# Seven half-width products for eight in w1 of the SwiGLU: Strassen's scheme on 18 of 22 feature tiles

## The chip, the cores and the metric

The kernel runs on one core of a Trainium2 chip. A core has engines that run side by side and wait for each other through semaphores: TensorE (PE in the profile; PEld is its weight load), VectorE (DVE), ScalarE (ACT), GpSimd (POOL) and the engine that issues most of the DMAs (SP). Matmul results land in PSUM, which is used here as eight banks of 128 x 512 fp32; everything else that is held on chip lies in SBUF. The metric is the device time of one execution in microseconds (us).

## The reference

One layer of a diffusion backbone over 512 tokens of width 1024: a modulated RMSNorm, two parallel token mixers (mLSTM and Hyena), a gated merge and an output projection with a residual; then the part that matters here:

```python
x = x + g1 * y
h2 = rmsnorm(x, norm2_g[l]) * (1.0 + sc2) + sh2
x = x + g2 * swiglu(h2, ffn_w1[l], ffn_w3[l], ffn_w2[l])
return rmsnorm(x, final_g)

def swiglu(h, w1, w3, w2):
    return (jax.nn.silu(h @ w1) * (h @ w3)) @ w2
```

Here w1 and w3 are 1024 x 2816 and w2 is 2816 x 1024; all data are fp32.

## The kernel before, in words

Everything is kept transposed: features on the 128 partitions, the 512 tokens along the free axis. The model width is 8 tiles (KT) of 128 features, the hidden width of the SwiGLU 22 tiles (FT).

Precision. Each fp32 operand is split into a rounded high part and the rest, hi and lo (`split`, L214 to L216: ScalarE copies hi, VectorE subtracts to get lo). A product is three matmuls, hi x hi, hi x lo and lo x hi, accumulated in PSUM (`mm3`, L233 to L236). `gemm` (L574) runs `mm3` over eight 128-row blocks: 24 matmuls of a 128 x 128 stationary block against 128 x 512 moving columns. `wsplit` (L240) loads a weight tile into a buffer "wr" and splits it into buffers "wh" and "wl"; each of these tags has four buffers.

Order. The program text lists the work; a planner fixes, before the run, the order of the instructions of each engine's queue. It takes from the instructions whose inputs and buffers are free by its own estimate the one that stands earliest in the text. `wsplit` runs under a raised priority: its load and split count as 600 instructions earlier. `behind()` ties a block's instructions behind an earlier matmul.

The stages around the change:

- The output projection. `out_tile` (L1478) forms x1 (the residual stream, 8 tiles of 128 x 512), which stays in the two big "K" buffers to the end of the kernel. The last four tiles are made for one half of the tokens and then for the other (`last_tile`, L1520: matmuls 256 columns wide).
- The second norm. `norm2(hf)` (L1526) scales x1 by the norm (L1534, into scratch), adds the shift on ScalarE for the high part of h2 (L1535) and on VectorE for its low part (L1539), one half of the tokens at a time.
- The lead. w1 and w3 of feature tiles 0 and 1 are multiplied half by half of the tokens, 256 columns wide (`high_first`, L1550; L1556).
- The feature loop (L1584). For each of the 22 tiles, `up` (L1576) gives the products with w1 and w3 (for tiles 0 and 1 those of the lead), then L1588 to L1590 form silu(a) * b, L1598 splits it into hi and lo, and `background()` does one step of the modulation vectors that are needed last (one weight load, one VectorE pass, L363 and L373).
- The w2 loop (L1614). For each of 8 output tiles three loads of w2, 66 matmuls over the 22 hidden tiles, then `out_tile` and the final scale; the last output tile is made in two halves of the tokens, each followed by the last norm and the store (`last_norm`, L1603).

PSUM is two sets of four banks: `bank(psG)` for the gemms, `bank()` (psH) for the rest.

Of the kernel before, what the change touches and what calls it, by code (L numbers as in the profile page):

```python
# [9 lines left out]
F32 = mybir.dt.float32  # L10
F32R = mybir.dt.float32r
AF = mybir.ActivationFunctionType
# [5 lines left out]
SEQ = 512  # L18
# [142 lines left out]
def build(nc, tc, I, out, dbg=None):  # L161
# [40 lines left out]
    def bank(p=None):  # L202
        return T(p or psH, [128, 512], F32, "bank")
# [10 lines left out]
    def split(hi, lo, x):  # L214
        act.activation(hi, x, AF.Copy)  # L215
        dve.tensor_sub(lo, x, hi.bitcast(F32))  # L216
# [16 lines left out]
    def mm3(o, wh, wl, xh, xl, first, last):  # L233
        pe.matmul(o, wh, xh, start=first, stop=False)  # L234
        pe.matmul(o, wh, xl, start=False, stop=False)  # L235
        return pe.matmul(o, wl, xh, start=False, stop=last)  # L236
# [3 lines left out]
    def wsplit(src, shape):  # L240
        n = int(np.prod(shape[1:]))
        raw = T(PW, [128, WMAX], F32, "wr")
        hi = T(PW, [128, WMAX], F32R, "wh", 4)
        lo = T(PW, [128, WMAX], F32R, "wl", 4)

        def view(t):
            v = t[:, :n]
            return v if len(shape) == 2 else v.rearrange("p (a b) -> p a b", a=shape[1])

        with tc.high_priority(PR[0]):  # L250
            if isinstance(src, list):
                for s, sl in src:
                    dma(view(raw)[:, :, sl], s)
            else:
                dma(view(raw), src)
            split(hi[:, :n], lo[:, :n], raw[:, :n])
        return view(hi), view(lo)
# [928 lines left out]
    def background():  # L1186
        next(later, None)
# [155 lines left out]
    def steps(n):  # L1343
        for _ in range(n):
            background()
# [73 lines left out]


    PF = st.enter_context(pool("pf", reuse_waits="tile"))
    BUFS["big"] = 36
    g1h = T(P0, [128, KT], F32, "g1h")
    g2h = T(P0, [128, KT], F32, "g2h")
    am2 = T(P0, [128, KT], F32, "am2")
# [52 lines left out]
    def out_tile(ps, n, d, g, c0, x, xo, acc):  # L1478
        sl = slice(c0, c0 + n)
        dve.scalar_tensor_tensor(xo[:, sl], ps[:, :n], g[:, d : d + 1], x[:, sl], op0=ALU.mult, op1=ALU.add)  # L1480
# [39 lines left out]
    def last_tile(hf, d):  # L1520
        wh, wl = ws[d - KT + LAST]
        ps = bank(psG)
        gemm(ps, wh, wl, [half(t, hf) for t in y[0]], [half(t, hf) for t in y[1]], 256)
        return out_tile(ps, 256, d, g1h, 256 * hf, xr[d], x1[d], acc1)

    def norm2(hf, cols):  # L1526
        with behind():
            rb = half_rms(cols)
        ts = []
        for k in range(KT):  # L1530
            if k % 2 == 0:
                pair = scr()
            ts.append(half(pair, k % 2))
            m = dve.scalar_tensor_tensor(ts[k], half(x1[k], hf), am2[:, k : k + 1], rb[:, :256], op0=ALU.mult, op1=ALU.mult)  # L1534
            act.activation(half(h2[0][k], hf), ts[k], AF.Identity, bias=modT[:, 3, k, 0:1])  # L1535
        with tc.issue_after(m.ins):
            for k in range(KT):
                hi = half(h2[0][k], hf).bitcast(F32)
                dve.scalar_tensor_tensor(half(h2[1][k], hf), ts[k], modT[:, 3, k, 0:1], hi, op0=ALU.add, op1=ALU.subtract)  # L1539
# [7 lines left out]
    norm2(0, cols)  # L1547
    for d in range(KT - LAST + 2, KT):
        sq1 = last_tile(1, d)
    def high_first(ps, wh, wl, hf):  # L1550

        n = 0
        for w, x in ((wh, 0), (wl, 0), (wh, 1)):
            for k in range(KT):
                n += 1
                m = pe.matmul(ps, w[:, k], half(h2[x][k], hf), start=n == 1, stop=n == 3 * KT)  # L1556
        tails.append(m.ins)

    ff = ([], [])
# [24 lines left out]
    for f in range(FT):  # L1584
        pa = up("w1", f)
        pb = up("w3", f)
        t = scr()
        act.activation(t[:], pa[:], AF.Tanh, scale=0.5)  # L1588
        dve.scalar_tensor_tensor(t[:], t[:], 1.0, pa[:], op0=ALU.add, op1=ALU.mult)
        dve.tensor_tensor(t[:], t[:], pb[:], op=ALU.mult)  # L1590
        if f < 4:
            pair = T(PT, [128, 2, SEQ], F32R, ("uh", "ul")[f % 2])
            hl = pair[:, 0], pair[:, 1]
        else:
            hl = big(), big()
        for i in range(2):
            ff[i].append(hl[i])
        split(hl[0][:], hl[1][:], t[:])  # L1598
        background()
    dve.tensor_scalar_mul(g2h[:], modT[:, 5, :, 0], 0.5)  # L1600
    acc2 = scr()

# [8 lines left out]
    def half2(o, d, hf):  # L1611
        return o[:, d : d + 2, 256 * hf : 256 * hf + 256]

    for d in range(KT):  # L1614
        ws = []
        for k0 in (0, 8, 16):
            n = min(8, FT - k0)
            wh, wl = wsplit(I["w2"][d, :, k0 : k0 + n], [128, n, 128])
            ws += [(wh[:, k], wl[:, k]) for k in range(n)]
        for c0, n in ((0, SEQ),) if d < KT - 1 else ((0, 256), (256, 256)):  # L1620
            ps = bank(psG)
            sl = slice(c0, c0 + n)
            for k in range(FT):
                mm3(ps[:, :n], ws[k][0], ws[k][1], ff[0][k][:, sl], ff[1][k][:, sl], k == 0, k == FT - 1)
            sq = out_tile(ps, n, d, g2h, c0, x1[d], x1[d], acc2)
            act.activation(x1[d][:, sl], x1[d][:, sl], AF.Copy, scale=fing[:, d : d + 1])
            if n < SEQ:
                last_norm(c0 // 256, sq)
    st.close()
# [16 lines left out]
```

## Time and profile before

| | |
|---|---|
| median of 3 runs | 1216.29 us (1215.84 to 1220.05) |
| the profiled execution | 1217.14 us, its span 1215.2 us |
| mean granted TensorE clock | 0.995 |
| busy share of the span | PE 97%, PEld 83%, DVE 69%, ACT 43%, POOL 7% |
| second norm and lead | to 864.7 us |
| feature loop beyond the lead | 864.7 to 1082.3 us |
| w2 loop, last norm | 1082.3 to 1215.2 us |

The span is the time from the first instruction to the last. In rows of the timeline the columns are start and duration in us, the engine, the line of the kernel, the operation, its output and input by the program's names, and in brackets the idle time before it and what ended that. The duration of one row overlaps the start of the next on the same engine, so the cost of an instruction in a busy stretch is the distance of the starts.

### The profile page before, as it was taken

What the parts mean: (1) busy time and instruction counts of PE and PEld (TensorE: products, weight loads), DVE (VectorE), ACT (ScalarE), POOL (GpSimd) and SP (SyncE); (2) the same over time, 40 slices, a digit from 0 to 9 for tenths busy, and PEclk for the clock granted to TensorE, in tenths of its full rate; (3) what the DMA queues carried; (4) which work ended last, traced back from release to release, by engine and by line L of the source; (5) the groups of instructions that cost most, each with busy time, mean ns of one, the idle gap of its engine ahead of it and who ended that gap; (6) DMA issues with size and microseconds to landing.
All of it is one profiled execution on the core that took longest, in us unless ns stands there. A gap on an engine that the chain in (4) does not pass through costs nothing.

```text
span 1215.2 us, 16927 instructions
## 1 busy us (share of the span) xinstructions
PE 1180.2 (97%) x6488; PEld 1014.5 (83%) x6488; DVE 833.1 (69%) x1338; ACT 528.6 (43%) x825; POOL 88.4 (7%) x168
## 2 busy tenths in 40 slices
PE   4999999999999999999999999999999999999997
PEld 2799988888888888888889898779988888888886
DVE  6967797978989999898668786776753434432332
ACT  3754465753545444454666542233432232322221
POOL 0011110100010010101032221000000000000000
PEclk9999999999999999999999999999999999999999
DMA  9744353364244352435575677783543323233312
GB/s 349 247 161 161 137 184 106 135 240 141 74 161 139 127 177 94 150 112 176 200 235 196 204 234 251 257 286 97 153 151 104 93 99 102 85 95 96 96 48 70
DMA packets 63377, 189.04 MB, mean 156 GB/s; under 512 B 8760, under 2 KB 12608, under 8 KB 61120
## 3 DMA queue, kind: packets, MB, share of 16 engines
q1 hardware_dynamic: 51536, 150.20, 38.1%
q0 software_dynamic: 11760, 37.76, 8.7%
q8 instruction: 51, 0.84, 0.3%
q14 instruction: 30, 0.25, 0.1%
HBM read 154.37 MB, written 33.55 MB: 155 GB/s over the span
## 4 chain that ended last, share of the span: by engine, by line
PE 82%; DVE 8%; DMA 5%; issue 2%; ACT 2%; POOL 0%; SPq 0%; DVEq 0%; POOLq 0%; ACTq 0%
PE bank L234 23%; PE bank L235 23%; PE bank L236 23%; DMA wr<-in_wada 2%; PE bank L661 2%; PE bank L660 2%; PE bank L662 2%; PE bank L1556 2%; DMA wr<-in_wph 1%; DVE wl L216 1%; DVE wr L373 1%; PE bank L617 1%; PE bank L464 1%; PE bank L465 1%; DMA ul<-in_xT 1%
## 5 line engine op out<-in xcount | busy, mean ns | idle before, releaser
L234 PE MATMUL bank<-hTh,wh 128*128 128x512 f32 x896 | 351.1, 393 | 2.0 <-ACT hTh L1112 2.0
L235 PE MATMUL bank<-hTl,wh 128*128 128x512 f32 x896 | 350.6, 391 | 2.2 <-DVE hTl L1118 2.2
L236 PE MATMUL bank<-hTh,wl 128*128 128x512 f32 x896 | 350.1, 391 | 0.0
L215 ACT ACTIVATE wh<-wr 128x1024 fp32r<-128x1024 f32 (+1 forms) x167 | 172.2, 1032 | 406.4 <-PE bank L235 197.9
L216 DVE TENSOR_TENSOR wl<-wr,wh 128x1024 fp32r<-128x1024 f32 (+1 forms) x167 | 198.1, 1189 | 172.9 <-ACT wh L215 171.4
L234 PEld LDWEIGHTS bank<-hTh,wh 128*128 128x128 f32 x896 | 168.8, 188 | 35.9 <-ACT hTh L1112 2.2
L235 PEld LDWEIGHTS bank<-hTl,wh 128*128 128x128 f32 x896 | 168.8, 188 | 35.5 <-DVE hTl L1118 2.5
L236 PEld LDWEIGHTS bank<-hTh,wl 128*128 128x128 f32 x896 | 168.7, 188 | 34.4
L234 PE MATMUL bank<-big,wh 128*128 128x512 f32 (+1 forms) x274 | 97.0, 354 | 1.3 <-ACT big L215 1.3
L235 PE MATMUL bank<-big,wh 128*128 128x512 f32 (+1 forms) x274 | 97.0, 354 | 0.6 <-DVE big L216 0.6
L236 PE MATMUL bank<-big,wl 128*128 128x512 f32 (+1 forms) x274 | 96.6, 353 | 0.0
L234 PEld LDWEIGHTS bank<-big,wh 128*128 128x128 f32 x274 | 52.1, 190 | 8.6 <-ACT big L215 1.7
L235 PEld LDWEIGHTS bank<-big,wh 128*128 128x128 f32 x274 | 52.3, 191 | 8.0 <-DVE big L216 1.1
L373 DVE SCALAR_TENSOR_TENSOR wr<-wr,crow 128x1024 f32<-128x1024 f32 x32 | 38.9, 1220 | 29.0 <-DMA wr<-in_wada 29.0
L236 PEld LDWEIGHTS bank<-big,wl 128*128 128x128 f32 x274 | 52.3, 191 | 6.9
L215 ACT ACTIVATE hb<-hb 128x512 fp32r<-128x512 f32 (+1 forms) x49 | 36.6, 768 | 32.2 <-DVE hb L469 17.5
L1590 DVE TENSOR_TENSOR s<-s,bank 128x512 f32<-128x512 f32 x22 | 15.1, 686 | 48.1 <-PE bank L236 48.1
L392 POOL TENSOR_TENSOR rr<-rv,negh 128x2 f32<-128x2 f32 (+1 forms) x6 | 5.5, 924 | 511.3 <-DVE rv L390 511.3
L216 DVE TENSOR_TENSOR hb<-hb,hb 128x512 fp32r<-128x512 f32 (+1 forms) x49 | 40.5, 860 | 2.0 <-ACT hb L215 1.8
L660 PE MATMUL bank<-wh,hTh 128*128 128x256 f32 (+1 forms) x128 | 36.5, 285 | 0.0
L662 PE MATMUL bank<-wh,hTl 128*128 128x256 f32 (+1 forms) x128 | 36.5, 285 | 0.0
L661 PE MATMUL bank<-wl,hTh 128*128 128x256 f32 (+1 forms) x128 | 36.4, 284 | 0.0
(390 smaller groups left out, 2259.7 us busy)
## 6 DMA issues: line engine op xcount, KB each, us to landing
wr<-in_win SPq DMA_DIRECT2D x64, 512.0 KB, 4.0
wr<-in_w SPq DMA_DIRECT2D x60, 512.0 KB, 3.6
wr<-in_wada SPq DMA_DIRECT2D x32, 512.0 KB, 4.2
Kd<-K POOLq DMA_DIRECT2D x8, 1024.0 KB, 4.7
K<-Kd SPq DMA_DIRECT2D x8, 1024.0 KB, 6.4
wr<-in_wv SPq DMA_DIRECT2D x8, 512.0 KB
gmd<-s POOLq DMA_DIRECT2D x16, 256.0 KB, 2.6
wr<-in_wph SPq DMA_DIRECT2D x8, 512.0 KB, 3.9
```

Of the source, the lines that this page charges most:

```text
L215: act.activation(hi, x, AF.Copy)
L216: dve.tensor_sub(lo, x, hi.bitcast(F32))
L234: pe.matmul(o, wh, xh, start=first, stop=False)
L235: pe.matmul(o, wh, xl, start=False, stop=False)
L236: return pe.matmul(o, wl, xh, start=False, stop=last)
L373: dve.scalar_tensor_tensor(w, w, 1.0, crow[:], op0=ALU.mult, op1=ALU.mult, accum_out=s)
L464: pe.matmul(ps[:], lhs, w4h, start=True, stop=False)
L660: pe.matmul(o, xh, wh, start=bool(k == 0), stop=False)
L661: pe.matmul(o, xh, wl, start=False, stop=False)
L662: m = pe.matmul(o, xl, wh, start=False, stop=bool(k == KT - 1))
L1556: m = pe.matmul(ps, w[:, k], half(h2[x][k], hf), start=n == 1, stop=n == 3 * KT)
L1590: dve.tensor_tensor(t[:], t[:], pb[:], op=ALU.mult)
```

## The change

w1 of feature tiles 4 to 21 is done in nine pairs of tiles. The product of a pair is seen as a 2 x 2 block product: two feature tiles (rows of the result) by two halves of the tokens (columns), summed over two halves of the 1024 inputs. Strassen's scheme in the form with common sub-sums (Winograd's) needs seven block products where the plain way needs eight; each block product is four 128-row blocks, three matmuls each, 256 columns wide.

- `input_sums` (once, after feature tile 1) forms the four sums of quarter blocks of h2 from the scaled values, which `norm2` now leaves in eight buffers (`scaled`), and splits them into hi and lo.
- `weight_sums` (each pair) loads the two w1 tiles, forms four sums of weight blocks in place, and splits the seven stationary blocks: p (A11, A12), q (A22), u (S3, S4), v (S1, S2). These four take all four buffers of "wh" and "wl". It is not under the raised priority.
- `pair_up` runs the seven products into four banks of psH and puts the results together: one copy on ScalarE, four sums on VectorE, into a "K" buffer.
- silu(a) * b is kept unsplit (`raw`) and split later: four tiles within the feature loop, the other 18 (`ff_split`) in the w2 loop.
- The first two output tiles of w2 are done together, hidden tile by hidden tile, into two banks.
- x1 is stored to DRAM (`x1d`) and loaded back in the w2 loop, so that the "K" buffers are free between. The tag "big" has 38 buffers in place of 36. `background()` runs once a pair.

w3, feature tiles 0 to 3 and the output tiles 2 to 7 are computed as before.

```diff
+    x1d = T(PD, [128, KT, SEQ], F32, "x1d")
...
     def project(d, ps):
         out_tile(ps, SEQ, d, g1h, 0, xr[d], x1[d], acc1)
+        store(x1d[:, d], x1[d])
...
+    scaled = [big(F32) for _ in range(KT)]
...
-        ts = []
+        ts = [half(t, hf) for t in scaled]
...
+    store(x1d[:, KT - LAST :], xq[1][:])
...
+    def input_sums():
+        sh = modT[:, 3, :, 0]
+        dsh = T(PF, [128, KH], F32, "dsh", 1)
+        dve.tensor_sub(dsh[:], sh[:, KH:], sh[:, :KH])
+        for k in range(KH):
+            (l0, l1), (h0, h1) = ([half(scaled[j], i) for i in range(2)] for j in (k, k + KH))
+            dve.tensor_sub(l0, l1, l0)
+            dve.scalar_tensor_tensor(l1, h1, dsh[:, k : k + 1], l1, op0=ALU.add, op1=ALU.subtract)
+            dve.scalar_tensor_tensor(h1, h1, sh[:, k + KH : k + KH + 1], l0, op0=ALU.add, op1=ALU.subtract)
+            dve.scalar_tensor_tensor(h0, h0, sh[:, k + KH : k + KH + 1], h1, op0=ALU.add, op1=ALU.subtract)
...
+        for k in range(KT):
...
+            split(hi, lo, scaled[k_][:])
...
+    def weight_sums(n, f):
...
+        dma(r1[:, : 2 * H], I[n][f].rearrange("p a b -> p (a b)"))
+        dma(r2[:, : 2 * H], I[n][f + 1].rearrange("p a b -> p (a b)"))
+        a11, a12, a21, a22 = r1[:, :H], r1[:, H : 2 * H], r2[:, :H], r2[:, H : 2 * H]
...
+        p, q, u, v = pair(), pair(), pair(), pair()
+        split(p[0][:, : 2 * H], p[1][:, : 2 * H], r1[:, : 2 * H])
+        split(q[0][:, :H], q[1][:, :H], a22)
+        dve.tensor_tensor(a11, a11, a21, op=ALU.subtract)
+        dve.tensor_tensor(a21, a21, a22, op=ALU.add)
+        dve.tensor_tensor(a22, a22, a11, op=ALU.subtract)
+        dve.tensor_tensor(a12, a12, a22, op=ALU.subtract)
+        split(u[0][:, : 2 * H], u[1][:, : 2 * H], r1[:, : 2 * H])
+        split(v[0][:, : 2 * H], v[1][:, : 2 * H], r2[:, : 2 * H])
...
+    def pair_up(n, f, ts):
+        w = weight_sums(n, f)
...
+        b = [bank() for _ in range(4)]
+        for a, x, o in (("a11", b11, half(b[0], 0)), ("a12", b21, half(b[1], 0)), ("a22", ts[3], half(b[2], 0)), ("s3", ts[2], half(b[3], 0)),
+                        ("s4", b22, half(b[3], 1)), ("s1", ts[0], half(b[2], 1)), ("s2", ts[1], half(b[1], 1))):
+            for k in range(KH):
+                m = mm3(o, w[a][0][k], w[a][1][k], x[0][k], x[1][k], k == 0, k == KH - 1)
...
+        act.activation(c[:, 6], half(b[0], 0), AF.Copy)
+        dve.tensor_tensor(c[:, 0:5:4], two(b[1]), twice(6), op=ALU.add)
+        dve.tensor_tensor(c[:, 5:7], two(b[3]), twice(4), op=ALU.add)
+        dve.tensor_tensor(c[:, 2:4], two(b[2]), twice(5), op=ALU.add)
+        dve.tensor_tensor(c[:, 1], half(b[2], 1), c[:, 6], op=ALU.add)
...
+    for f in range(LEAD, FT, 2):
+        t = [silu_half(a) for a in pair_up("w1", f, ts)]
+        b = [up("w3", f + i)[:] for i in range(2)]
+        for i in range(2):
+            gated(t[i], b[i])
+        if early < EARLY and f > LEAD:
+            for _ in range(1):
+                ff_split(early, big()[:], big()[:])
+                early += 1
         background()
...
+    pair = [bank() for _ in range(2)]
+    for k0 in (0, 8, 16):
+        ws = [w2_part(d, k0) for d in range(2)]
+        for k in range(k0, min(k0 + 8, FT)):
+            if ff[0][k] is None:
+                ff_split(k, *next(free))
+            for d in range(2):
+                m = mm3(pair[d][:], *ws[d][k - k0], ff[0][k][:], ff[1][k][:], k == 0, k == FT - 1)
+        if k0 < 16:
+            reload_x1(k0 // 8)
```

In the w2 loop the split parts of hidden tiles 4 to 11 go to the buffers of h2 (`hTh`, `hTl`), those of 12 to 17 to "big", those of 18 to 21 to "uh" and "ul".

More of the change, by code (lines that the diff above doesn't have):

```diff
@@ L1557, in high_first @@
         tails.append(m.ins)
-    ff = ([], [])
+    ff, raw = ([None] * FT, [None] * FT), []
     lead = {}
@@ L1585, in build @@
+    LEAD, EARLY = 4, 4
+    for f in range(LEAD):
         pa = up("w1", f)
         pb = up("w3", f)
[L1587 to L1595, printed above, removed]
-        for i in range(2):
-            ff[i].append(hl[i])
@@ L1600, in build, with places @@
+    def places():
+        for _ in range(KT):
+            yield slots("hTh")()[:], slots("hTl")()[:]
+        for _ in range(FT - EARLY - KT - 4):
+            yield big()[:], big()[:]
+        for _ in range(2):
+            u, v = (T(PT, [128, 2, SEQ], F32R, t) for t in ("uh", "ul"))
+            for j in range(2):
+                yield u[:, j], v[:, j]
+    free = places()
+    x1.clear()
+    xq = [T(PT, [128, 4, SEQ], F32, "K") for _ in range(2)]
     dve.tensor_scalar_mul(g2h[:], modT[:, 5, :, 0], 0.5)
@@ L1612, in half2, with w2_part, reload_x1, down_tile @@
         return o[:, d : d + 2, 256 * hf : 256 * hf + 256]
[L1614 to L1619, printed above, removed]
+    def w2_part(d, k0):
+        n = min(8, FT - k0)
+        wh, wl = wsplit(I["w2"][d, :, k0 : k0 + n], [128, n, 128])
+        return [(wh[:, k], wl[:, k]) for k in range(n)]
+    def reload_x1(i):
+        store(xq[i][:], x1d[:, 4 * i : 4 * i + 4])
+        x1.extend(xq[i][:, j] for j in range(4))
+    pair = [bank() for _ in range(2)]
[8 more added lines that the diff above has]
+            reload_x1(k0 // 8)
+    tails.append(m.ins)
+    def down_tile(d, ps, c0, n):
+        sl = slice(c0, c0 + n)
+        sq = out_tile(ps, n, d, g2h, c0, x1[d], x1[d], acc2)
+        act.activation(x1[d][:, sl], x1[d][:, sl], AF.Copy, scale=fing[:, d : d + 1])
+        return sq
+    for d in range(2):
+        down_tile(d, pair[d], 0, SEQ)
+    for d in range(2, KT):
+        ws = [w for k0 in (0, 8, 16) for w in w2_part(d, k0)]
         for c0, n in ((0, SEQ),) if d < KT - 1 else ((0, 256), (256, 256)):
```

51 lines of the change are left out of this document (43 added, 8 removed).

## The prediction

> **What bounds the kernel now.** I read the page first: the busy shares, then the chain that ended last.
>
> ```profile
> span 1215.2 us, 16927 instructions
> PE 1180.2 (97%) x6488; PEld 1014.5 (83%) x6488; DVE 833.1 (69%) x1338; ACT 528.6 (43%) x825; POOL 88.4 (7%) x168
> PE 82%; DVE 8%; DMA 5%; issue 2%; ACT 2%; POOL 0%; SPq 0%; DVEq 0%; POOLq 0%; ACTq 0%
> ```
>
> TensorE carries 82% of the chain. The shares are means over stages, so the second view is the busy time in stretches: the half-width products of the output projection, the feature loop, and the w2 loop (columns: stretch, length, busy time and count of PE, PEld, DVE, ACT, POOL, granted clock, DMA share, GB/s).
>
> ```profile
> 822.00:836.00 14.00, 14.00 (x120) 14.00 (x119) 6.50 (x14) 4.05 (x8) 1.74 (x1) 1.00 0.12 39
> 865.00:1082.00 217.00, 217.00 (x959) 179.74 (x958) 92.95 (x113) 62.58 (x80) 0.00 (x0) 1.00 0.36 111
> 1082.00:1195.00 113.00, 113.00 (x532) 94.94 (x531) 34.11 (x36) 30.48 (x36) 0.00 (x0) 1.00 0.25 73
> ```
>
> In the feature and w2 loops PE has no gap at full clock, while VectorE is busy 43% and 30% of the time. So time is won there by taking matmul time away and lost by making PE wait. The third view is the order in time, for the pace. One turn of the feature loop on VectorE:
>
> ```profile
> 1049.90 0.69 DVE L1590 TENSOR_TENSOR s<-s,bank 128x512 f32<-128x512 f32 x1 [2.70 <-PE bank L236]
> 1050.81 1.22 DVE L216 TENSOR_TENSOR wl<-wr,wh 128x1024 fp32r<-128x1024 f32 x1 [0.23 <-ACT wh L215]
> 1051.95 0.69 DVE L216 TENSOR_TENSOR big<-s,big 128x512 fp32r<-128x512 f32 x1
> 1056.25 1.23 DVE L216 TENSOR_TENSOR wl<-wr,wh 128x1024 fp32r<-128x1024 f32 x1 [3.61 <-ACT wh L215]
> 1057.39 0.68 DVE L1589 SCALAR_TENSOR_TENSOR s<-s,bank 128x512 f32<-128x512 f32 x1
> 1060.78 0.69 DVE L1590 TENSOR_TENSOR s<-s,bank 128x512 f32<-128x512 f32 x1 [2.70 <-PE bank L236]
> ```
>
> L1590 waits for the second gemm of a turn, and it comes every 10.88 us: 48 matmuls of 512 columns, 0.2267 us each. VectorE has two waits of 2.7 and 3.6 us in each turn. The half-width pace is read from the output projection's last tiles, where L1480 waits for a gemm of 24 matmuls of 256 columns:
>
> ```profile
> 821.14 0.49 DVE L1480 SCALAR_TENSOR_TENSOR K<-bank,g1h,big 128x256 f32<-128x256 f32 x1 [1.42 <-PE bank L236]
> 824.02 0.49 DVE L1480 SCALAR_TENSOR_TENSOR K<-bank,g1h,big 128x256 f32<-128x256 f32 x1 [1.48 <-PE bank L236]
> 826.90 0.48 DVE L1480 SCALAR_TENSOR_TENSOR K<-bank,g1h,big 128x256 f32<-128x256 f32 x1 [1.42 <-PE bank L236]
> ```
>
> 2.88 us for 24 is 0.120 us each: more than half of 0.2267 (0.1133). That surcharge eats much of what one product in eight saves. Each of these gemms has new weights, bank and waits, and the pace is still 2.88, so the start of a product costs nothing visible.
>
> **The change, part by part.**
>
> *Removed and added on PE.* Before, w1 of two tiles: 48 x 0.2267 = 10.88 us. After: 7 products x 4 blocks x 3 = 84 half-width matmuls, 84 x 0.120 = 10.08 us. Nine pairs save 9 x 0.80 = 7.2 us. w3 and w2 keep their matmuls.
>
> By the Trainium skill, "TensorE: Matmul & The Clock Gate", section "Back-to-back issue gap", a warm matmul of N columns is spaced N/2.4 + 2.5 ns: 215.8 and 109.2 ns, and the sum by it would be 9 x (48 x 0.2158 - 84 x 0.1092) = 10.7 us, an estimate. The trace's spacings are 11 ns above both; I go by the trace.
>
> *VectorE and ScalarE in a pair.* Distances of starts in busy stretches give the cost:
>
> ```profile
> 850.40 3.22 DVE L1534 SCALAR_TENSOR_TENSOR s<-K,am,bank 128x256 f32<-128x256 f32 x8 [1.70 <-PE bank L394]
> 853.54 3.25 DVE L1539 SCALAR_TENSOR_TENSOR hTl<-s,modT,hTh 128x256 fp32r<-128x256 f32 x8
> ...
> 898.32 1.23 DVE L373 SCALAR_TENSOR_TENSOR wr<-wr,crow 128x1024 f32<-128x1024 f32 x1 [3.17 <-DMA wr<-in_wada]
> 899.47 0.08 DVE L373 DVE_READ_ACCUMULATOR wr<-wr,crow 128x1 f32 x1
> 899.47 1.22 DVE L216 TENSOR_TENSOR wl<-wr,wh 128x1024 fp32r<-128x1024 f32 x1
> 900.61 0.68 DVE L1590 TENSOR_TENSOR s<-s,bank 128x512 f32<-128x512 f32 x1
> 901.20 0.16 DVE L376 TENSOR_TENSOR modT<-modT,vecs 128x8 f32<-128x8 f32 x1
> ```
>
> 1024 columns cost 1.14 us, 512 cost 0.6, 256 cost 0.4 (3.22 / 8). A pair then takes of VectorE: lo of p, q, u, v 3 x 1.14 + 0.6 = 4.0; four weight sums 2.4; two w3 tiles 2.3; four output sums 3 x 0.6 + 0.4 = 2.2; silu and gate 2.4; one early split 0.6; one modulation pass 1.2. That is 15.1 us in a pair of 10.08 + 10.88 = 20.96 us: 72%. No row shows a sum in place, or one that writes two separate blocks; the nearest, which reads a bank with a repeated operand (L1608), has 682 ns, as L1590 has without one (686). So I take the single cost; double, as the upper bound, adds 2.4 + 2.2 and gives 19.7 us, still under 20.96. On ScalarE the 1024-column copy has a mean of 1.06 us:
>
> ```profile
> L216 DVE TENSOR_TENSOR wl<-wr,wh 128x1024 fp32r<-128x1024 f32 x39 | 47.8, 1225 | 61.4 <-ACT wh L215 61.4
> L215 ACT ACTIVATE wh<-wr 128x1024 fp32r<-128x1024 f32 x39 | 41.4, 1061 | 139.0 <-issue 135.4 <-PE bank L235 2.0 <-PE bank L1556 0.8
> L1588 ACT ACTIVATE s<-bank 128x512 f32<-128x512 f32 x20 | 11.6, 582 | 0.0
> ...
> L1590 DVE TENSOR_TENSOR s<-s,bank 128x512 f32<-128x512 f32 x22 | 15.1, 686 | 48.1 <-PE bank L236 48.1
> L1608 DVE TENSOR_TENSOR s<-K,bank 128x512 f32<-128x512 f32 x8 | 5.0, 682 | 3.3 <-PE bank L394 3.3
> ```
>
> At most 5 x 1.06 + 6 x 0.6, 9 us of 20.96. All of it lies beside PE: cost 0 if the order lets it. If that cover goes, the price is the first rival below.
>
> *Weight buffers in a pair.* The order of needs is p, q, u, v, then w3 tiles a, b, with four buffers. If the buffers go round in this order, the next p and q take those of u and v, free when the seven products end, 10.9 us before they are needed. The next u takes a's, free 5.4 us before the pair starts; the next v takes b's, free only at its start, and is ready some 1.06 + 1.14 = 2.2 us later; it is read by the sixth product, 5 x 1.44 = 7.2 us in. a and b take p's and q's, free 2.9 and 4.3 us in, needed at 10.1. Nothing is late. That buffers go round in the text's order, whatever the priority, I read from the load queue, where the unraised modulation loads stand between the raised w1, w3 loads, one for each turn:
>
> ```profile
> 859.93 0.33 SPq L363 DMA_DIRECT2D wr<-in_wada  x1
> 861.67 3.03 SPq L255 DMA_DIRECT2D wr<-in_w  x2
> 866.72 0.33 SPq L363 DMA_DIRECT2D wr<-in_wada  x1
> 867.86 4.85 SPq L255 DMA_DIRECT2D wr<-in_w  x2
> ```
>
> *The first pair.*
>
> ```profile
> 864.71 0.40 PE L234 MATMUL bank<-hTh,wh 128*128 128x512 f32 x1
> ...
> 867.75 0.68 DVE L1590 TENSOR_TENSOR s<-s,bank 128x512 f32<-128x512 f32 x1
> ```
>
> From the end of norm2 (853.54 + 3.25 = 856.8) VectorE has until s3 is read. PE runs tiles 2 and 3 plainly from 864.7 for 4 x 5.44 us, to 886.4, and reaches s3 at 886.4 + 3 x 1.44 = 890.7. Work due by then: silu and gate of tiles 0 to 2 and the first half of 3, 4.2; four plain weight tiles 4.6; input sums 16 x 0.4 + 8 x 0.6 + 0.2 = 11.4; p, q, sums and u 5.2. Together 25.4 of 33.9 us. I take 0; if the planner starts the input sums only after the gate of tile 1 (868.4 in this trace) they end at 879.8 and u still fits. Bound 0 to 2 us.
>
> *w2, first two tiles together.* 132 matmuls either way, 29.9 us. The splits moved here take 0.6 on VectorE and ScalarE per hidden tile against 6 x 0.2267 = 1.36 on PE; four are made before, so the fifth is due 5.4 us in, and its buffer falls free in the last w3 gemm. Cost 0. Without that head start the first would cost about 1.2 us once.
>
> *x1 through DRAM.* Five stores and two loads on POOL's queue.
>
> ```profile
> 71.57 0.72 POOL L509 DMA_DIRECT2D Kd<-K  x1 [10.35 <-DVE K L508]
> ...
> 853.19 1.72 PE L1556 MATMUL bank<-hTh,wh 128*128 128x256 f32 x13
> ...
> 848.78 0.70 POOL L392 TENSOR_TENSOR rr<-rv,negh 128x2 f32<-128x2 f32 x1 [16.22 <-DVE rv L390]
> Kd<-K POOLq DMA_DIRECT2D x8, 1024.0 KB, 4.7
> ```
>
> The 1 MB store becomes ready some 846 us in and holds POOL about 0.7 us; the power of the second norm (L392), queued behind it, is due at 848.8, and PE's wait behind that is covered until 853.2, when it turns to the second half of the tokens. Cost 0; at worst 0.7. The loads back have 15 us and more for 4.7.
>
> *Sum.* 1217.14 (the profiled execution, 1.9 above its span) - 7.2 = 1209.9. The median, 1216.29, is 0.85 lower: 1209.1 us. A median run can tell some 0.5%, 6.1 us, from no change, so the gain stands only 1.1 us beyond that.
>
> **The rivals.**
>
> *First, slower: the weight sums come late in every pair.* They are not raised, and stand in the text after the gate of the pair before, which waits for the last w3 gemm. If VectorE kept the text's order, PE would wait at each pair's start for that gate and lo of p, 0.6 + 1.14, and again at s3: p, q, four sums end 4.8 us in, hi of u 5.8, lo 7.0, when PE has been ready since 1.7 + 4.3 = 6.1. That is 2.6 us a pair, 9 x 2.6 = 24, net 17: 1233 us. It costs the gain from 0.8 us a pair on, and decides for "slower" from 1.5. Against it:
>
> ```profile
> 845.41 1.22 DVE L373 SCALAR_TENSOR_TENSOR wr<-wr,crow 128x1024 f32<-128x1024 f32 x1
> ...
> 846.89 1.22 DVE L373 SCALAR_TENSOR_TENSOR wr<-wr,crow 128x1024 f32<-128x1024 f32 x1
> ```
>
> These two passes belong to the feature loop (eight L373 rows from here on are its eight) and are not raised, yet run before the norm2(1) rows at 850.4, which stand earlier in the text. Work that is ready is drawn ahead. For the rival: the planner goes by its own estimate of durations, and its queues don't change when the chip is otherwise.
>
> *Second, same: the order is right but for single waits* at the first pair, at v, or at the start of w2, together 2 to 5 us: 1211 to 1214, say 1213. For it: VectorE goes from 43% to 72%, and every buffer of "wh" is in use.
>
> *Third, faster still:* the surcharge of half-width matmuls is not theirs but due to a stream in those stretches (PEld is busy 14.00 of 14.00 there) and absent here. Then 84 x 0.1133 = 9.52 us a pair, 9 x 1.36 = 12.2: 1204. Against it: the same 0.120 in all the half-width gemms.
>
> *Fourth: the change doesn't do what it says*, since the larger "big" tag moves buffers and the planner orders earlier stages otherwise:
>
> ```profile
> 700.00:818.00 118.00, 114.70 (x590) 97.53 (x589) 89.58 (x177) 37.62 (x58) 12.53 (x23) 0.99 0.76 256
> ```
>
> PE idles 3.3 us in the stage before the half-width products, so I give this 3 us either way, inside the range and within the cases above.
>
> **How the numbers follow.** Forecast 0.48 (its own range 1208.5 to 1211, from -7.7 to -5.3), third rival 0.04, second rival 0.32, first 0.16, of which a quarter is a light form (1 us a pair, 1218). Faster: 0.04 and all of the forecast but some 0.02 that falls short of 6.1 us, and a few hundredths of the second: 0.52. Slower 0.14, same 0.34. Range 1207 to 1222: it leaves out the third rival and the heavy part of the first, 0.17.
>
> **What would show it.** Right: in the feature loop PE busy throughout, turns of 20.96 us per pair, 84 half-width matmuls in 10.08; VectorE near 72% there; the w2 loop starting 7.2 us earlier and as long as before. Wrong: idle PE at the start of a pair with VectorE's weight split as the releaser (first rival), idle PE once near 886 to 895 or at the start of w2 (second), 0.113 per half-width matmul (third).

## The result, and the profile after

The changed kernel takes 1210.22 us (median of 6 runs, 1209.88 to 1210.75), the kernel before beside it 1216.07 us (6 runs, 1214.89 to 1220.05). The ratio of the means is 0.9945, with a 95% interval from 0.9927 to 0.9963: 0.55% faster, 4.5 to 8.9 us. The forecast was 1209.1 us, 7.2 us less than before.

The page of the changed kernel: span, busy shares, and the chain that ended last.

```profile
span 1208.6 us, 17766 instructions
PE 1174.4 (97%) x6812; PEld 1024.5 (85%) x6812; DVE 901.4 (75%) x1453; ACT 552.6 (46%) x860; POOL 92.2 (8%) x175
PE 85%; DVE 6%; DMA 5%; issue 2%; ACT 1%; POOL 0%; SPq 0%; DVEq 0%; POOLq 0%; ACTq 0%
```

TensorE has 324 matmuls more, 9 x (84 - 48), and is busy 5.8 us less. VectorE has 68 us of work more, and its share of the chain fell from 8% to 6%: the added sums are not on the path that sets the end.

The busy time of the changed kernel in stretches (columns as in the prediction): the feature loop, the seven products of the first pair, the two w3 tiles behind them, and most of the w2 loop.

```profile
865.00:1075.00 210.00, 210.00 (x1283) 189.32 (x1282) 155.93 (x217) 82.92 (x107) 1.11 (x2) 1.00 0.39 127
886.52:896.59 10.07, 10.07 (x85) 10.06 (x84) 7.14 (x8) 4.62 (x5) 0.00 (x0) 1.00 0.76 237
896.59:907.50 10.91, 10.91 (x50) 9.02 (x49) 7.89 (x13) 2.85 (x4) 0.00 (x0) 1.00 0.21 70
1075.00:1190.00 115.00, 115.00 (x549) 96.91 (x548) 41.24 (x50) 35.13 (x47) 0.00 (x0) 1.00 0.26 82
```

PE has no gap in either loop, at full clock. The 84 half-width matmuls take 10.07 us, 0.120 us each, and the two w3 tiles 10.91. In one pair VectorE is busy 7.14 + 7.89 = 15.03 of 20.98 us, 72%.

The pace of the pairs is read from ScalarE's copy of the first product (L1671), which comes once a pair. These are its rows in the first two pairs and the last:

```profile
888.15 0.38 ACT L1671 ACTIVATE K<-bank 128x256 f32<-128x256 f32 x1 [0.54 <-PE bank L236]
909.13 0.38 ACT L1671 ACTIVATE K<-bank 128x256 f32<-128x256 f32 x1 [0.54 <-PE bank L236]
...
1055.99 0.38 ACT L1671 ACTIVATE K<-bank 128x256 f32<-128x256 f32 x1 [0.54 <-PE bank L236]
```

(1055.99 - 888.15) / 8 = 20.98 us a pair, and the first is no different from the rest. Before, two feature tiles took 21.76 us.

The first matmuls of the feature loop and of the w2 loop, in the order of time of TensorE, the kernel before first and the changed kernel second:

```profile
864.71 0.40 PE L234 MATMUL bank<-hTh,wh 128*128 128x512 f32 x1
...
1082.34 0.39 PE L234 MATMUL bank<-uh,wh 128*128 128x512 f32 x1
```

```profile
864.73 0.40 PE L234 MATMUL bank<-hTh,wh 128*128 128x512 f32 x1
...
1075.34 0.39 PE L234 MATMUL bank<-big,wh 128*128 128x512 f32 x1
```

The loop fell from 217.63 to 210.61 us, by 7.02 = 9 x 0.78. It starts at the same time in these two executions (0.02 us apart), so the stages before it cancel. From the start of the w2 loop to the end of the execution the kernel before takes 134.80 us (1217.14 - 1082.34) and the changed one 135.07 (1210.41, its profiled execution, - 1075.34): 0.27 given back, nearly all of it behind the last product, in the last norm and its store. Together 0.02 - 7.02 + 0.27 = -6.73 us between the two profiled executions.

### The profile page after: what moved, and what is told of

It reads as the page before. It is cut to its first block, busy times and chain, and to the rows that moved or that the text cites. A ratio compares the mean times of both kernels' runs of the same rounds, so it can differ in the third digit from the quotient of the medians.

```text
span 1208.6 us, 17766 instructions
## 1 busy us (share of the span) xinstructions
PE 1174.4 (97%) x6812; PEld 1024.5 (85%) x6812; DVE 901.4 (75%) x1453; ACT 552.6 (46%) x860; POOL 92.2 (8%) x175
## 4 chain that ended last, share of the span: by engine, by line
PE 85%; DVE 6%; DMA 5%; issue 2%; ACT 1%; POOL 0%; SPq 0%; DVEq 0%; POOLq 0%; ACTq 0%
PE bank L234 24%; PE bank L235 24%; PE bank L236 24%; DMA wr<-in_wada 3%; PE bank L1558 2%; PE bank L661 2%; PE bank L662 2%; PE bank L663 2%; DVE wl L216 1%; DVE wr L373 1%; PE bank L617 1%; PE bank L464 1%; DMA wr<-in_win 1%; PE bank L465 1%; PE bank L882 1%
## 5 line engine op out<-in xcount | busy, mean ns | idle before, releaser
L234 PE MATMUL bank<-hTh,wh 128*128 128x512 f32 (+1 forms) x932 | 352.2, 379 | 2.0 <-ACT hTh L1113 2.0
L235 PE MATMUL bank<-hTl,wh 128*128 128x512 f32 (+1 forms) x932 | 351.5, 377 | 1.9 <-DVE hTl L1119 1.9
L236 PE MATMUL bank<-hTh,wl 128*128 128x512 f32 (+1 forms) x932 | 350.9, 376 | 0.0
L215 ACT ACTIVATE wh<-wr 128x1024 fp32r<-128x1024 f32 (+3 forms) x185 | 187.2, 1014 | 343.7 <-PE bank L235 260.2
L216 DVE TENSOR_TENSOR wl<-wr,wh 128x1024 fp32r<-128x1024 f32 (+3 forms) x185 | 214.5, 1164 | 124.7 <-ACT wh L215 123.0
L235 PE MATMUL bank<-big,wh 128*128 128x256 f32 (+1 forms) x274 | 90.3, 330 | 0.6 <-DVE big L216 0.6
L234 PE MATMUL bank<-big,wh 128*128 128x256 f32 (+1 forms) x274 | 90.4, 330 | 0.0
L236 PE MATMUL bank<-big,wl 128*128 128x256 f32 (+1 forms) x274 | 90.1, 329 | 0.0
L215 ACT ACTIVATE hb<-hb 128x512 fp32r<-128x512 f32 (+1 forms) x49 | 36.5, 767 | 32.3 <-DVE hb L469 17.5
L216 DVE TENSOR_TENSOR hb<-hb,hb 128x512 fp32r<-128x512 f32 (+1 forms) x49 | 40.4, 860 | 2.0 <-ACT hb L215 1.8
L234 PE MATMUL bank<-uh,wh 128*128 128x256 f32 (+1 forms) x124 | 39.8, 321 | 0.0
L235 PE MATMUL bank<-ul,wh 128*128 128x256 f32 (+1 forms) x124 | 39.8, 321 | 0.0
L236 PE MATMUL bank<-uh,wl 128*128 128x256 f32 (+1 forms) x124 | 39.8, 321 | 0.0
```

## The experiments

The theory: the gain is matmul time taken off an otherwise full TensorE, 0.8 us a pair; everything else lies beside it, because work that is ready is drawn ahead. The rivals: the weight sums decide a pair's start; the rest of the change moves the time too; VectorE is near its limit.

**The change without its pairs.** All 22 feature tiles are computed plainly; the stores of x1, the late splits of the hidden tiles and the first two w2 tiles together stay. The input sums are left out.

```diff
-    LEAD, EARLY = 4, 4
+    LEAD, EARLY = FT, 4
...
-        if f == 1:
-            ts = input_sums()
+        if f >= 6 and f % 2 == 0 and f <= 12:
+            ff_split((f - 6) // 2, big()[:], big()[:])
+        if f % 2 == 1:
+            background()
```

> The changed kernel with all 22 feature tiles of w1 done plainly (no weight sums, no input sums, no seven products); x1 through DRAM, the late splits and the joint first two w2 tiles stay. Theory (the whole gain is matmul time: nine pairs at 10.88 - 10.10 = 0.78 us): 9 x 0.78 = 7.0 us above the changed kernel, about 1217, as the kernel before. Rival (part of the gain comes from the other parts): clearly under 1215.

Measured: 1216.64 us, ratio 0.9996 [0.9987, 1.0006]. The feature loop in its stretch:

```profile
865.00:1082.00 217.00, 217.00 (x959) 179.75 (x958) 88.66 (x108) 59.29 (x74) 0.00 (x0) 1.00 0.37 116
```

The same 959 matmuls in the same 217 us as in the kernel before. From its first matmul to the first of the w2 loop, the feature loop takes 217.63 us here as in the kernel before. The DRAM detour, the late splits and the doubled w2 tiles cost and bring nothing; the gain is that of the seven products.

**Five pairs in place of nine** (feature tiles 12 to 21).

```diff
-    LEAD, EARLY = 4, 4
+    LEAD, EARLY = 12, 4
...
+        if f >= 5 and f % 2 == 1:
+            background()
```

> The changed kernel with tiles 4 to 11 plain and five pairs (12 to 21) in place of nine. Theory: 4 x 0.78 = 3.1 us above the changed kernel, 1213.3, pairs still 20.98 us apart. Rival (a fixed cost of the sums, paid once, hides part of a larger gain per pair): more than 4 us above, since the gain per pair would be larger than 0.78.

Measured: 1214.38 us, ratio 0.9970 [0.9957, 0.9984]. ScalarE's copies of the first product, the first two of five:

```profile
973.20 0.39 ACT L1671 ACTIVATE K<-bank 128x256 f32<-128x256 f32 x1 [0.54 <-PE bank L236]
994.18 0.39 ACT L1671 ACTIVATE K<-bank 128x256 f32<-128x256 f32 x1 [0.54 <-PE bank L236]
```

Again 20.98 us apart. Five ninths of 0.55% is 0.31%, and 0.30% was measured. That interval is wide (0.16% to 0.43%), but the trace is sharper: from its first matmul to the first of the w2 loop the feature loop takes 213.73 us, 3.90 = 5 x 0.78 less than before. The gain grows with the number of pairs, with no fixed price for the first.

**The first rival made: the weight sums in the text's order.** VectorE's part of a pair's weight sums, the low parts and the four sums, is tied behind the last gate of the tiles before; the loads and ScalarE's copies are not.

```diff
-        t = [silu_half(a) for a in pair_up("w1", f, ts)]
+        with tc.issue_after(last):
+            w = weight_sums("w1", f)
+        t = [silu_half(a) for a in pair_up(w, ts)]
...
-            gated(t[i], b[i])
+            last = gated(t[i], b[i])
```

> The changed kernel with the VectorE work of each pair's weight sums queued behind the gate of the tile before it, as the text stands. Theory (the order on VectorE is what keeps TensorE fed): TensorE waits at each pair's start for the gate and the low part of p, and again at s3, 2.6 us a pair, 24 in all: 1234. Rival (buffers and the slack of VectorE cover it): 1210 to 1213.

Measured: 1241.07 us, ratio 1.0189 [1.0173, 1.0205]. What TensorE waits for in this kernel (us in total, times, longest):

```profile
PE bank L236 <- DVE wl L216: 14.3, 10, 1.8
PE bank L234 <- ACT wh L215: 7.9, 14, 0.7
```

The place is the forecast one: TensorE stands at the start of a pair for VectorE's low part of the weights, and later for ScalarE's high part of the sums. Of the first line 1.1 us, one wait, lie ahead of the feature loop, and that wait stands in the changed kernel too; in the changed kernel's feature loop neither line appears. The sums of the next pair stand there ahead of the gate that the text has before them. From VectorE's order in time of the changed kernel (L1642 is a weight sum of the next pair, L1672 an output sum of this one, L1595 the gate):

```profile
1022.02 0.69 DVE L1642 TENSOR_TENSOR wr<-wr,wr 128x512 f32<-128x512 f32 x1
...
1023.36 0.68 DVE L1672 TENSOR_TENSOR K<-bank,K 128x512 f32<-128x512 f32 x1
...
1033.58 0.69 DVE L1595 TENSOR_TENSOR big<-s,bank 128x512 f32<-128x512 f32 x1 [3.08 <-PE bank L236]
```

The price was larger than forecast. Eight pairs, from 894.04 to 1089.10 us, take 195.06 us, 24.4 each, 3.4 more than in the changed kernel, where 2.6 had been worked out. Where the rest comes from is seen at the longest wait, in TensorE's order in time:

```profile
939.23 0.28 PE L235 MATMUL bank<-ul,wh 128*128 128x256 f32 x1
941.31 0.38 PE L236 MATMUL bank<-hTh,wl 128*128 128x256 f32 x1 [1.81 <-DVE wl L216]
941.53 0.28 PE L234 MATMUL bank<-hTh,wh 128*128 128x256 f32 x1
...
943.22 0.41 PE L235 MATMUL bank<-hTl,wh 128*128 128x256 f32 x1
943.43 0.41 PE L236 MATMUL bank<-hTh,wl 128*128 128x256 f32 x1
```

A wait costs more than its idle time. From start to start it takes 2.08 us in place of 0.12, and the matmul behind it another 0.22 in place of 0.12: 1.81 us of idle time cost 2.06. That surplus of 0.25 us is called the restart here; with three stops in a pair it adds some 0.75 us. And one us after this wait the matmuls come every 0.21 us. TensorE's stretches there: 3.4 us from 1 us behind this wait on, the stretch from this pair's copy of the first product (L1670 in this kernel) to the next, and the same of a late pair (columns: stretch, length, PE's busy time and count, granted clock, DMA share, GB/s).

```profile
942.40:945.80 3.40, 3.40 (x19) 0.51 0.00 0
...
943.03:968.34 25.31, 23.50 (x134) 0.90 0.30 104
...
1065.01:1089.10 24.09, 21.75 (x134) 1.00 0.39 132
```

The granted clock is 0.51 behind that wait, and 0.90 from copy to copy, because a second stretch of 3.4 us at half rate begins before the end (at 966.2 us). The late pair, at full clock, has 24.09 - 21.75 = 2.34 us of idle time, near the forecast 2.6, and is 3.11 longer than 20.98; the restarts are the difference. The eight pairs together are 27.2 us longer than 8 x 20.98: 18.8 us are idle (195.06 less 176.24 busy), 20 restarts are some 5.0, and the two stretches at half rate 3.4. The clock does not fall behind every wait: of the four waits of 1.81 us in this kernel two are followed by half rate (those that end at 941.31 and 965.99 us) and two are not (990.68 and 1015.36). The Trainium skill, "TensorE: Matmul & The Clock Gate", section "Part 1: The HAM clock gate", says that the array falls back to half its clock after an idle window of about 3.4 us and is released after about as long a busy one, on a window that runs freely. The trace agrees with the half rate and with its coming only at some waits, but shows it behind an idle time of 1.81 us already, and in the w3 kernel below not behind one of 2.10 + 0.45 us: the length of a wait alone does not decide it.

**VectorE filled with other work.** Eight, and in another kernel fourteen, products of a scratch tile of 512 columns with itself are added in each pair.

```diff
+        for _ in range(8):
+            dve.tensor_tensor(idle[:], idle[:], idle[:], op=ALU.mult)
```

> The changed kernel with eight more VectorE products of 128 x 512 in each pair, on a buffer that nothing else uses: 8 x 0.6 = 4.8 us on top of 15.2 in a pair of 20.98, 95%. Theory (VectorE's work lies wholly beside TensorE): the time stays, 1210 to 1211. Rival (the slack is in pieces that the waits bound, and cannot be used up): TensorE waits for weight splits, 1214 or more.

> The changed kernel with fourteen more VectorE products of 128 x 512 in each pair: 15.2 + 8.4 = 23.6 us in a pair of 20.98. Theory: VectorE becomes the bound of the feature loop, 9 x 2.6 = 24 us more, 1234. Rival (the planner lets the added work fall behind into the w2 loop, where VectorE has 60% to spare): much less than 24.

Measured: 1216.47 us with eight, ratio 0.9986 [0.9978, 0.9995], and 1217.65 in one run with fourteen. Nearly the whole gain is lost, but not in the pairs. The stretch of the output projection, in the changed kernel first and with eight products second:

```profile
700.00:818.00 118.00, 115.82 (x593) 98.36 (x592) 90.98 (x180) 39.11 (x60) 14.69 (x27) 0.99 0.80 268
```

```profile
700.00:818.00 118.00, 112.44 (x563) 95.26 (x564) 105.89 (x206) 38.44 (x58) 14.59 (x28) 0.97 0.79 264
```

```profile
L1677 DVE TENSOR_TENSOR idle<-idle x72: 680/691/696, 750.5 to 922.6; 128x512 f32<-128x512 f32 x72
```

The added work depends on nothing, so it was drawn ahead too: its 72 rows lie from 750.5 to 922.6 us, while the pairs run from about 893 to 1082. In the output projection VectorE was 77% busy already (90.98 of 118 us); with the added rows it is 90% busy, and PE does 3.4 us less there. The feature loop itself takes 210.61 us with eight and with fourteen, as in the changed kernel; it only starts later, at 871.48 and 872.11 us in place of 864.73. These runs do not test what they were meant to. One thing can still be read from the kernel with fourteen, in the stretch of one of its pairs; the first seven look alike, with VectorE busy for 20.67 to 20.88 us:

```profile
895.53:916.51 20.98, 20.98 (x134) 19.09 (x133) 20.67 (x31) 7.48 (x9) 0.00 (x0) 1.00 0.37 125
```

VectorE is busy 99% of these pairs, TensorE has no gap, and the pair still takes 20.98 us. Within a pair, work that can be put anywhere fills VectorE to the brim without harm. What happens when the work has a place in the chain of a pair is the question of the w3 runs below.

**The weight sums on GpSimd**, all four of a pair.

```diff
-        dve.tensor_tensor(a11, a11, a21, op=ALU.subtract)
+        gp.tensor_tensor(a11, a11, a21, op=ALU.subtract)
...
```

> The changed kernel with the four weight sums of each pair on GpSimd in place of VectorE. Theory (TensorE sets the pace, and the sums are far ahead of their need): the same 1210, VectorE 2.4 us less busy in a pair. The rows of GpSimd's sums give their price. Rival (GpSimd's sums are so slow, over some 2 us each, that s3 and s4 come late): 1213 or more.

Measured: 1211.08 us, ratio 0.9950 [0.9936, 0.9964], pairs again 20.98 apart: the same as the changed kernel. Groups of GpSimd's sums (count, busy time and mean in ns) and, in the same kernel, of VectorE's work beside them (for L1590 the shortest, middle and longest row in ns); then, in order of time, VectorE's two rows of L1590 in the first pair and the GpSimd sum that they meet:

```profile
L1643 POOL TENSOR_TENSOR wr<-wr 128x512 f32<-128x512 f32 x9 | 15.2, 1684 | 0.7
...
L1644 POOL TENSOR_TENSOR wr<-wr,wr 128x512 f32<-128x512 f32 x9 | 11.6, 1293 | 0.7
```

```profile
L1590 DVE SCALAR_TENSOR_TENSOR s<-s,K x18: 685/727/1781, 902.9 to 1072.7; 128x512 f32<-128x512 f32 x18
...
L216 DVE TENSOR_TENSOR wl<-wr,wh 128x512 fp32r<-128x512 f32 x8 | 9.3, 1167 | 1.5 <-ACT wh L215 1.5
...
L1672 DVE TENSOR_TENSOR K<-bank,K 128x512 f32<-128x512 f32 x9 | 6.2, 689 | 3.8 <-PE bank L236 3.8
```

```profile
902.92 2.41 DVE L1590 SCALAR_TENSOR_TENSOR s<-s,K 128x512 f32<-128x512 f32 x2 [0.70 <-ACT s L1589]
...
903.16 1.62 POOL L1645 TENSOR_TENSOR wr<-wr,wr 128x512 f32<-128x512 f32 x1
```

Four sums that cost VectorE 2.4 us take GpSimd about 6, and where a VectorE row reads two buffers of SBUF, the two engines hold each other up. The first row of L1590 had begun when L1645 starts, and takes 0.71 us, near the 0.69 of the changed kernel; L1645 takes 1.62 us where a sum of GpSimd's that meets no such row (L1644) takes 1.29. The second row starts within L1645 and takes 1.78 us, so that the two take 2.41 us where they take 1.29 in the changed kernel. It is the same in the first eight pairs. The mean of L216 with 512 columns goes from 681 to 1167 ns. L1672, which reads a PSUM bank and SBUF, keeps its time (683 and 689). By the Trainium skill, "SBUF — State Buffer", section "Who interferes with whom", a VectorE instruction with two SBUF inputs contends with a GpSimd instruction that reads SBUF, and one with at most one, outside VectorE's two-port modes, does not; the trace agrees in both halves. Here there is room for it, so it costs nothing, and frees nothing either.

**w3 by seven products too**, for all nine pairs, with the sums on VectorE; and the same with the weight sums on GpSimd.

```diff
-        t = [silu_half(a) for a in pair_up("w1", f, ts)]
-        b = [up("w3", f + i)[:] for i in range(2)]
+        t = [silu_half(a) for a in pair_up("w1", f, ts, psH)]
+        b = pair_up("w3", f, ts, psG)
```

> The changed kernel with w3 of tiles 4 to 21 by the same seven products too, sums on VectorE. TensorE would need 2 x 10.10 = 20.2 us for a pair of tiles, 0.78 less; VectorE 12.8 for two sets of weight parts, 4.4 output sums, 2.4 silu and gate, 0.6 and 1.2 for the early split and the modulation pass, 21.4. Theory (VectorE becomes the bound): pairs of 21.4 us or more, so 9 x 0.4 = 4 us above the changed kernel or more, 1214 to 1220. Rival (TensorE still sets the pace): 1203.

> As with w3 by seven products too, but the eight weight sums of a pair of tiles on GpSimd: VectorE 16.6 us against 20.2 on TensorE. Theory: pairs of 20.2 us, 9 x 0.78 = 7.0 us under the changed kernel, 1203.2, if a sum on GpSimd takes under some 1.5 us. Rival (the wait between GpSimd's sums and the splits behind them, with only four weight buffers and no plain product between, leaves TensorE waiting): 1210 or more.

Measured: 1218.69 us, ratio 1.0005 [0.9994, 1.0015], with the sums on VectorE, and 1269.34 us, ratio 1.0421 [1.0406, 1.0436], with them on GpSimd. Nine more sets of seven should have brought another 7 us, and a loop of 203.6 us (210.6 - 7.0). The w3 kernel with VectorE's sums: its feature loop from the first matmul to the first of the w2 loop, and, engine by engine, one of its four stalls, on ScalarE, VectorE and TensorE.

```profile
861.25:1081.48 220.23, 211.55 (x1610) 204.73 (x1609) 206.49 (x299) 95.53 (x133) 0.08 (x1) 0.98 0.34 112
```

```profile
984.96 1.15 ACT L1589 ACTIVATE s<-K 128x512 f32<-128x512 f32 x2 [1.63 <-DVE K L1675]
986.01 3.45 ACT L215 ACTIVATE wh<-wr 128x1024 fp32r<-128x1024 f32 x4
...
984.84 0.68 DVE L1645 TENSOR_TENSOR wr<-wr,wr 128x512 f32<-128x512 f32 x1
...
987.11 0.39 PE L234 MATMUL bank<-big,wh 128*128 128x256 f32 x1 [1.33 <-ACT wh L215]
988.05 0.58 PE L234 MATMUL bank<-big,wh 128*128 128x256 f32 x1 [0.44 <-ACT wh L215]
988.43 0.41 PE L235 MATMUL bank<-big,wh 128*128 128x256 f32 x1
```

The time with the sums on VectorE lies in the range that was expected, but not for the reason that was given. From w1's copy (L1671) to the next, four of eight pairs take 20.1 to 20.9 us, less than the 21.4 of VectorE's load, and four take 23.3 to 24.2: it is stalls that cost, with VectorE 94% busy (206.49 of 220.23 us), because every piece of its work now has a place. ScalarE's copy of this set's high weights u (L215) stands in its queue behind the tanh (L1589), which waits for VectorE's last output sum (L1675). The copy also needs the last weight sum (L1645), which VectorE does only after that, from 984.84 to about 985.5 us: without the tanh ahead of it the copy could have begun only some 0.5 us earlier. TensorE waits 1.33 + 0.44 us for the copies, and then runs at half pace (rows of 0.41 us from 988.43 on). The set lasts 13.88 us in place of 10.08: some 2 us of the 3.8 are the wait, the rest is the clock. Over the loop TensorE is idle for 8.7 us (220.23 - 211.55), and three stretches of 3.4 us at half pace cost some 5 more; the restarts and shorter delays make up the rest. With the sums on GpSimd the copy waits for them, 123.7 us in all between 890 and 1110 us, as the group of L215, what TensorE waits for in that kernel, and its feature loop show:

```profile
L215 ACT ACTIVATE wh<-wr 128x1024 fp32r<-128x1024 f32 x47 | 47.9, 1049 | 132.3 <-POOL wr L1645 123.7 <-PE bank L235 8.6
```

```profile
PE bank L234 <- ACT wh L215: 26.3, 14, 3.5
PE bank L236 <- DVE wl L216: 12.8, 18, 1.1
```

```profile
868.01:1138.73 270.72, 232.69 (x1611) 221.78 (x1609) 196.43 (x225) 91.86 (x131) 111.06 (x72) 0.90 0.28 92
```

Four sums in a row, some 6 us on GpSimd, stand between the first three weight blocks and the last four, and a set of seven lasts 10. The slower sums that were free with one set a pair now lie on the path. The loop is 67 us longer than 203.6: TensorE is idle for 38.0 us of them (270.72 - 232.69), and most of the rest is the clock, granted at 0.90, a tenth of 270.72 us. This expectation missed by more than any other here.

**w3 by seven products where there is room.** The two kernels above say that two sets fit a pair by VectorE's total but not every time. In the next kernel every other pair (tiles 6, 10, 14, 18) has w3 by seven; another does w1 of tiles 2 and 3 by seven as well, w3 of these first; a third adds w3 of tile pair 20 to the first. The changed kernel ran beside them once more. In the diff the last edit is the second kernel's alone.

```diff
-        b = [up("w3", f + i)[:] for i in range(2)]
+        b = pair_up("w3", f, ts, psG) if f in (6, 10, 14, 18) else [up("w3", f + i)[:] for i in range(2)]
...
-    LEAD, EARLY = 4, 4
+    LEAD, EARLY = 2, 4
```

> The changed kernel as it is, on the chip on which its variants run: 1210 to 1211, 0.9945 of the kernel before. It is there to compare the other three with.

> The changed kernel with w3 of four pairs of tiles (from 6, 10, 14, 18) by the seven products too, no two pairs next to each other; all sums on VectorE. VectorE needs 15.2 us in the five plain-w3 pairs and 21.4 in the four others, a mean of 18 against 20.6 on TensorE. Theory (VectorE costs nothing as long as its work of two neighbouring pairs fits, which it did at 99% busy): 4 x 0.78 = 3.1 us under the changed kernel, 1207. Rival (the chain gate, next weight buffer, split, product is too short of time where no plain product stands between two sets of seven, whatever VectorE's load): 3.8 us lost at each, so 1214 or more.

> As with w3 of four pairs by seven products, and w1 of tiles 2 and 3 too, ten pairs in place of nine; there w3 stands before w1 so that the input sums have 10.9 us more. VectorE has 21.3 us of work due in the 23.1 us before s3 is read. Theory: another 0.78 us less, 1206. Rival (input sums late): a wait of 1 us or more at the first pair, 1207 or more.

> As with w3 of four pairs, and the last pair (tiles 20, 21) too, which makes two neighbours. Theory (neighbours ask more of VectorE, 19.7 of 20.2 us without early split and modulation pass, than its order can give): no more than 0.4 us below the run with four. Rival: 0.78 below it.

| kernel | median, us | ratio to before | feature loop, us |
|---|---|---|---|
| changed, again | 1209.90 | 0.9934 [0.9921, 0.9948] | 210.61 |
| w3 of four pairs | 1205.69 | 0.9904 [0.9889, 0.9919] | 207.33 |
| and w1 of tiles 2, 3 | 1205.59 | 0.9901 [0.9885, 0.9916] | 207.33 |
| w3 of five pairs | 1204.77 | 0.9893 [0.9878, 0.9908] | 206.50 |

The last column is the time from the first matmul of feature tile 2 to the first of the w2 loop in the profiled execution. It tells the three apart, which the medians with their intervals don't. Two neighbouring pairs of the kernel with four, one with w1 alone and one with both:

```profile
909.63:950.77 41.14, 41.14 (x302) 39.25 (x301) 36.63 (x52) 17.73 (x23) 0.00 (x0) 1.00 0.37 121
```

41.14 us where the changed kernel has 2 x 20.98 = 41.96: each set more is worth its 0.8 us (210.61 - 207.33 = 4 x 0.82), TensorE has no gap, and VectorE, at 89%, has a plain pair in which to catch up. The theory held, and its rival fell. In the second kernel the tenth set of w1 brought nothing. Its first set on TensorE, from its first matmul to that of the next set (length, busy time and count, granted clock, DMA share, GB/s), and ScalarE's copies within it:

```profile
873.56:884.44 10.88, 10.44 (x85) 1.00 0.47 143
```

```profile
876.76 3.48 ACT L215 ACTIVATE wh<-wr 128x1024 fp32r<-128x1024 f32 x4 [1.19 <-DVE wr L1645]
```

ScalarE waits for the last weight sum (L1645), TensorE for ScalarE, 0.44 us once, and with the restart the set lasts 10.88 us in place of 10.08, which is all that it should have brought. The rival had the place right: VectorE is late at the first pair. Five sets of w3, the last of them in the last pair, take another 0.83 us off the loop: here the rival held, and the theory, that neighbours ask more than VectorE's order can give, did not. This is the version with the lowest median, 1.1% under the kernel before. Its feature loop:

```profile
865.00:1072.00 207.00, 207.00 (x1468) 195.59 (x1467) 183.13 (x259) 90.78 (x121) 0.58 (x1) 1.00 0.37 122
```

## Why the prediction was right, point by point

*The term of the sum* (nine pairs of 0.80 us) was right to 0.02 us a pair: the seven products take 10.07 us where 10.08 was said, the w3 tiles 10.91 where 10.88 was said, and a pair saves 0.78. That this term is the whole gain is shown by the run without pairs (nothing) and the one with five (five ninths: 3.90 of 7.02 us of the loop).

*VectorE and ScalarE hidden.* 72% was said and 72% came. The unknown cost, a sum in place or into two blocks, is the single one. The groups by form on VectorE in the changed kernel (L1642 in place, L1672 into two blocks):

```profile
L1672 DVE TENSOR_TENSOR K<-bank,K 128x512 f32<-128x512 f32 x9 | 6.1, 683 | 0.0
...
L1642 DVE TENSOR_TENSOR wr<-wr,wr 128x512 f32<-128x512 f32 x8 | 5.5, 692 | 0.3
```

*The first pair* was said to cost nothing, with a bound of 2 us. The low part of u of the first pair on VectorE, and the first matmul of s3 (which reads u) on TensorE, in order of time:

```profile
884.67 1.23 DVE L216 TENSOR_TENSOR wl<-wr,wh 128x1024 fp32r<-128x1024 f32 x1 [1.46 <-ACT wh L215]
...
890.83 0.28 PE L234 MATMUL bank<-big,wh 128*128 128x256 f32 x1
```

u is ready at 885.9, 4.9 us before its use; the prediction had 890.7 for the use, and 8.5 us to spare. *Weight buffers, w2 and x1 through DRAM* were costed at nothing and cost nothing: no wait of TensorE in either loop, and the run without pairs, which keeps the stores and the w2 part, is as fast as before.

*The rivals.* The first was priced at 2.6 us a pair: its idle time measures 2.3, but it costs 3.4, because each wait also has a restart (0.25 us) and some bring the half clock, two steps that the prediction did not have. What spoke against it (ready work is drawn ahead) is what the order of the changed kernel shows. The second did not come: no single wait. The third falls: 84 matmuls in 10.07 us. Its condition did not come either, since PEld is busy for 10.06 of these 10.07 us, as in the half-width products of before; whether the surcharge belongs to the width or to the weight loads beside it, no run here separates. The fourth did not show: the feature loop starts 0.02 us later than before. That is luck in part, since in the other kernels without added work, whose text ahead of the loop is the same, it starts anywhere from 861.25 to 868.68 us.

*The mis-sized terms* are small. The sum against the profiled execution was 1209.9, and 1210.41 came: 0.2 us in the nine pairs and 0.3 from the w2 loop on. And the step from the profiled execution to the median, 0.85 us taken off after three runs, is 0.2 in the changed kernel. The runs of the kernel before spread over 5 us (1214.89 to 1220.05), those of the changed one over 1, so the medians differ by 5.85 us, the profiled executions by 6.73, and the medians of the second time (ratio 0.9934) by 7.9. The time given, 1209.1, was 1.1 us too low. That the gain stands only just beyond what can be told from no change was right: the first interval still holds 0.5%, the second no longer.

## What to carry to other kernels

When TensorE has no gap, price an algorithm with fewer products by the pace of its narrower matmuls in the same trace: here the 6% surcharge of half-width matmuls (0.120 against half of 0.227) leaves 0.8 us of the 1.36 that one product in eight is worth. Work on other engines is free while the planner can move it to where there is room; work with a fixed place in a chain is not free even when the totals fit, so count the instructions between a result and its next use, and what stands in the queue in front of them. A wait of TensorE costs more than its length, through the restart and, at times, the clock behind it. Differences of 0.8 us, which medians of runs can't tell apart, stand plainly in the time of the one loop that was changed.

## What the runs showed of the hardware that was not expected

- After two of four TensorE waits of 1.81 us in the text-order kernel, and in the w3 kernel with VectorE's sums after all three waits of 1.33 us with one of 0.44 or 0.45 right behind, half-width matmuls came every 0.21 us for some 3.4 us, at about half the clock (granted 0.51 from 942.4 to 945.8 us in the text-order kernel). After a wait of 2.10 us with one of 0.45 behind in that w3 kernel the clock stayed at 1.00 (938 to 947 us), and so it did after the stops of 1.21, 0.69 and 0.45 us of a late pair of the text-order kernel.
- A stop of TensorE costs about 0.25 us beside its idle time: 2.06 us for 1.81, and some 5.0 of the 27.2 us in the eight pairs of the text-order kernel.
- GpSimd takes 1.29 us for a sum of 128 x 512 fp32 that takes VectorE 0.69. Beside VectorE's instructions with two SBUF inputs its sums take up to 2.83 us (L1642 at 876.60 us in the kernel with the sums on GpSimd), and such an instruction of VectorE's that starts within one of them up to 1.78; those that read a PSUM bank keep their 0.69.
- PEld is busy 10.06 of 10.07 us in the seven products, at 0.120 us a matmul, and 14.00 of 14.00 us in half-width gemms of before at the same pace.
